# Two decoder layers on one core: layer 0's block attention ahead of its sparse attention

## The chip, the core and the metric

The kernel runs on one core of one Trainium2 chip, as one program with one launch. The metric is the device time in microseconds (us). Matrix products run on TensorE, elementwise work and reductions on VectorE, activations and some copies on ScalarE, a smaller share on GpSimd (POOL in the profile), and the weights come in by DMAs that SyncE (SP) issues.

## The reference, cut to what matters

The input has 256 tokens of 1024 float32 numbers. Two layers follow one another, each a mixer, a cross-attention to 256 memory tokens and a gated feed-forward part, each behind an RMS norm and added to the residual stream. What the change touches is the mixer of layer 0. It has one input projection, two groups of eight heads, and one output projection:

```python
def dsa_moba_mixer(h, positions, w_in, w_out, ...):
    aq, ak, av, iq, ik, iw, bq, bk, bv = _split(h @ w_in, AB_SIZES)
    aq = partial_rope(rms_norm(aq, a_q_norm), positions)
    ak = partial_rope(rms_norm(ak, a_k_norm), positions)
    iq = partial_rope(iq, positions)
    ik = partial_rope(ik, positions)
    o_a = dsa_attention(aq, ak, av, iq, ik, iw)
    bq = partial_rope(rms_norm(bq, b_q_norm), positions)
    bk = partial_rope(rms_norm(bk, b_k_norm), positions)
    o_b = moba_attention(bq, bk, bv)
    return jnp.concatenate([o_a, o_b], axis=-1) @ w_out

def dsa_attention(q, k, v, q_idx, k_idx, w_idx):
    logits = einsum('bqhd,bsd->bqhs', q_idx, k_idx)
    score = einsum('bqh,bqhs->bqs', w_idx, relu(logits))
    score = where(causal, score, NEG_INF)
    _, sel = lax.top_k(score, 64)
    ...
```

Group A is the sparse attention. A small indexer of eight heads scores every key for every query, the 64 best keys are kept, and the eight heads attend to these through one shared key and value head. Group B is the block attention. With 256 tokens there is one block of 256 keys, so it is causal attention with eight key and value heads. The two groups need nothing of one another; their outputs meet in the output projection, whose rows 0 to 511 belong to A and 512 to 1023 to B.

## The kernel before, in words

**Tiles.** The tokens are two tiles (t = 0, 1) of 128. A gemm (L571) multiplies one token tile by one block of up to 512 weight columns into one of two PSUM buffers `mm`. Weights and activations are each split into a high and a low part of the type fp32r, and each product is three matmuls (`mm3`, L565): high by high, high by low, low by high. Eight slices of the 1024 inputs make 24 matmuls of 512 columns for one tile and one block; `both` (L588) runs the two tiles one after the other.

**Weights.** The list `plan` names the order in which weight pieces are loaded; it is filled from `BL0` (L413) for layer 0's input projection and goes on with `mk` (the memory's keys), the output projection `out` in two halves of 512 rows (half 0 is A's, half 1 is B's), `mq`, `mv`, `mo` and the feed-forward part. One piece is 2 slices by up to 512 columns. SyncE loads it into one of three buffers `raw`; `pusher` (L395) then casts it to the high part (mostly on ScalarE) and takes the low part by a subtraction on VectorE, into one of six buffers `whl`. Both token tiles use a piece before its buffer is free. In the trace this subtraction is `whl<-raw,whl`; the prediction calls it a split.

**Layer 0's mixer** (`mixer0`, L750) has five blocks: `s` of 424 columns (shared key and value of A, index queries, keys and weights), `aq`, `bk`, `bq` and `bv` of 512 each. `BL0` and the gemms at the end of `mixer0` have them in this order. Behind each gemm runs an evacuation: `ev_small` (L761) for `s`, `ev_q` (L850) for `aq` and `bq`, `ev_k` (L869) for `bk`, `ev_v` (L892) for `bv`. They scale, rotate and transpose (PSUM buffers `tp`), and write high and low parts into `slab` tiles.

Three loops follow. `index` (L812) computes, tile by tile, the eight index heads' scores on TensorE, ReLU on ScalarE and the weighted sum on VectorE into `acc`. `top` (L839) then runs eight rounds of MAX8 and MATCH_REPLACE on VectorE, each of which takes eight keys out, and turns the result into a mask, `bias`. `attention` (L898) goes through four (group, tile) pairs, four pairs of heads in each. Per pair of heads (`scores`, L692): scores into `sp`; mask and row maximum on VectorE; exponential on ScalarE; scaling; transposes into `tp`; copy to `pt`; product with the values into `po`. `finish` (L741) copies `po` to the two slabs that the output projection reads.

```python
def attention():
    for br, t in ((0, 0), (0, 1), (1, 0), (1, 1)):
        if br == 0:
            yield has(("aqT", t))
            yield has("akT", 2)
            yield has(("bias", t))
```

`br` 0 is A, the sparse attention, and 1 is B. So A's first tile waits for the first tile's top-k, A's second for the second tile's.

**After the mixer** `main` (L1479) runs `mem_k` (block `mk`), then `project` (L1375), which takes half 0 of the output projection for both tiles and then half 1, each with two column blocks, then the cross-attention (`mq` first) and the feed-forward part. `mem_prep` (L1242), the norm and transposes of the memory, is started ahead of the `bv` gemms.

**What sets the order.** All of this is generators that yield one instruction at a time. When the program is built, `Steps` (L84) picks among the instructions that are ready: per engine, of those that could start within 0.03 us of the earliest, the one with the lowest rank. When something could start is estimated by `Est` (L140), with durations from `Engine.cost` (L236) and `Est.issue` (L194). On the chip each engine runs its own queue in the order so fixed. Every instruction is issued by one line, L232 (L237 in the changed kernel), so that the trace tells operations apart by the tiles' names.

## Time and profile before

| what | us |
|---|---|
| median of 3 runs | 803.23 (802.14 to 803.38) |
| the profiled execution | 801.81 |
| its span | 800.1 |
| TensorE busy in it | 766.0 |
| VectorE busy | 537.5 |
| ScalarE busy | 435.4 |

The profile is of one execution. The span runs from the first to the last instruction that it shows; the execution's own time is 1.7 us longer. Busy time is the time in which an engine has an instruction running. A row of the view in time has start, duration and the instruction (output tile, input tiles, shapes, data type), how many like it follow one another, and in brackets how long the engine was idle just before and which engine's work ended that. PEclk is TensorE's granted clock as a share of 2.4 GHz, so that 0.50 is 1.2 GHz.

### The profile page before, as it was taken

The numbers are of one execution on the slowest core, as the hardware profiler recorded it, in microseconds if no ns is written. First come the engines' busy times: TensorE is split into PE (matmuls) and PEld (weight loads), VectorE is DVE, ScalarE is ACT, GpSimd is POOL, SyncE is SP. The second block draws the span as 40 slices with busy tenths as digits, with TensorE's granted clock in tenths as the row PEclk, the third lists the DMA queues.
The fourth block names the chain that finished last, engine by engine and source line by source line (L and its number), as shares of the span: only waits on it lengthen the run. The fifth ranks groups of instructions, "written<-read, shape, count | busy, mean of one in ns | idle before, by whom it ended". The sixth has DMA issues, their size and how long they took to land.

```text
span 800.1 us, 11833 instructions
## 1 busy us (share of the span) xinstructions
PE 766.0 (96%) x4259; PEld 632.1 (79%) x4259; DVE 537.5 (67%) x1096; ACT 435.4 (54%) x816; POOL 130.9 (16%) x192
## 2 busy tenths in 40 slices
PE   6878999999999999999999988999999999999998
PEld 5766777888888888888878776878897888889886
DVE  6779998877655655545727798887868565646541
ACT  5666887565544434444526788864656334435430
POOL 1544332110000000000007463230200000000000
PEclk9999999999999999999999999999999999999999
DMA  7613334635565553887315632033635656546761
GB/s 221 208 55 112 134 124 122 181 119 159 158 191 179 168 186 119 240 251 224 116 56 148 210 112 81 1 103 110 184 105 146 198 184 180 167 141 209 225 184 52
DMA packets 69482, 121.27 MB, mean 152 GB/s; under 512 B 8420, under 2 KB 15664, under 8 KB 69424
## 3 DMA queue, kind: packets, MB, share of 16 engines
q1 hardware_dynamic: 69392, 120.53, 49.2%
q8 instruction: 33, 0.54, 0.3%
q14 instruction: 25, 0.20, 0.1%
q0 software_dynamic: 32, 0.00, 0.0%
HBM read 119.46 MB, written 1.05 MB: 151 GB/s over the span
## 4 chain that ended last, share of the span: by engine, by line
PE 83%; DVE 7%; ACT 4%; DMA 2%; issue 2%; POOL 1%; SPq 0%; POOLq 0%; ACTq 0%; DVEq 0%
PE mm L232 61%; PE po L232 12%; PE tp L232 7%; PE sp L232 3%; DVE whl L232 2%; DMA raw<-in_ab_w_in 1%; DMA raw<-in_ffn_w_in 1%; ACT sn L232 1%; ACT whl L232 1%; DVE slab L232 1%; DVE acc L232 1%; ACT slab L232 1%; DVE sn L232 1%; DVE t L232 1%; POOL sn L232 1%
## 5 line engine op out<-in xcount | busy, mean ns | idle before, releaser
L232 PE MATMUL mm<-whl,h 128*128 128x512 f32 (+3 forms) x1776 | 397.8, 379 | 8.5 <-DVE whl L232 6.9
L232 PEld LDWEIGHTS mm<-whl,h 128*128 128x128 f32 x1776 | 310.8, 189 | 68.0 <-DVE whl L232 8.9
L232 DVE TENSOR_TENSOR whl<-raw,whl 128x1024 fp32r<-128x1024 f32 (+3 forms) x232 | 270.9, 1170 | 116.6 <-ACT whl L232 112.4
L232 ACT ACTIVATE whl<-raw 128x1024 fp32r<-128x1024 f32 (+3 forms) x211 | 213.2, 1014 | 160.1 <-DMA raw<-in_ffn_w_in 38.4
L232 PE MATMUL mm<-whl,slab 128*128 128x512 f32 (+1 forms) x840 | 200.2, 376 | 0.9 <-DVE x L232 0.8
L232 PEld LDWEIGHTS mm<-whl,slab 128*128 128x128 f32 x840 | 140.6, 189 | 27.7 <-issue 2.4
L232 PE MATMUL po<-whl,slab 128*128 128x512 f32 x264 | 68.4, 396 | 0.0
L232 ACT ACTIVATE slab<-tp 128x256 fp32r<-128x256 f32 (+2 forms) x63 | 28.3, 471 | 56.3 <-PE tp L232 55.9
L232 PEld LDWEIGHTS po<-whl,slab 128*128 128x128 f32 x264 | 49.4, 188 | 11.4
L232 POOL TENSOR_TENSOR rh<-vh,mhalf 128x1 f32<-128x1 f32 x12 | 9.5, 794 | 293.6 <-DVE vh L232 283.1
L232 ACT ACTIVATE sn<-sn,mx 128x128 f32<-128x128 f32 (+1 forms) x96 | 42.7, 447 | 6.9 <-DVE mx L232 6.5
L232 PE MATMUL tp<-ident,t 128*128 128x128 f32 x224 | 34.8, 277 | 2.7 <-DVE slab L232 2.3
L232 PE MATMUL tp<-ident,sn 128*128 128x128 f32 (+1 forms) x180 | 30.9, 281 | 4.8 <-POOL sn L232 3.8
L232 DVE TENSOR_TENSOR x<-mm,x 128x512 f32<-128x512 f32 x36 | 24.6, 687 | 16.0 <-PE mm L232 15.9
L232 PEld LDWEIGHTS tp<-ident,t 128*128 128x128 f32 x224 | 27.1, 142 | 9.6 <-DVE slab L232 2.8
L232 ACT ACTIVATE pt<-tp 128x512 f32<-128x512 f32 (+2 forms) x51 | 27.0, 536 | 13.7 <-PE tp L232 11.8
L232 DVE CUSTOM_DVE_ANT_0 sn<-sp,cm,rq 128x128 f32<-128x128 f32 (+1 forms) x80 | 30.5, 410 | 4.9 <-PE sp L232 3.8
L232 POOL TENSOR_TENSOR sn<-sn,rc 128x512 f32<-128x512 f32 (+2 forms) x27 | 25.5, 944 | 43.5 <-DVE rc L232 28.6
L232 ACT ACTIVATE t<-mm,rh 128x512 f32<-128x512 f32 (+1 forms) x26 | 17.0, 654 | 27.0 <-PE mm L232 27.0
L232 PEld LDWEIGHTS tp<-ident,sn 128*128 128x128 f32 (+1 forms) x180 | 20.7, 141 | 11.6 <-POOL sn L232 5.2
L232 ACT ACTIVATE t<-mm 128x512 f32<-128x512 f32 (+2 forms) x46 | 23.7, 553 | 10.0 <-PE mm L232 8.0
L232 DVE SCALAR_TENSOR_TENSOR t<-mm,rh,t 128x512 f32<-128x512 f32 (+1 forms) x24 | 16.9, 704 | 18.2 <-PE mm L232 18.2
(200 smaller groups left out, 676.3 us busy)
## 6 DMA issues: line engine op xcount, KB each, us to landing
raw<-in_ffn_w_in SPq DMA_DIRECT2D x80, 512.0 KB, 3.8
raw<-in_ffn_w_out SPq DMA_DIRECT2D x44, 512.0 KB, 4.5
raw<-in_ab_w_in SPq DMA_DIRECT2D x16, 512.0 KB, 3.9
raw<-in_mem_w_kv SPq DMA_DIRECT2D x16, 512.0 KB, 4.0
raw<-in_nsa_w_in SPq DMA_DIRECT2D x16, 512.0 KB, 3.7
raw<-in_ab_w_out SPq DMA_DIRECT2D x8, 512.0 KB, 3.6
raw<-in_mem_w_q SPq DMA_DIRECT2D x8, 512.0 KB, 4.2
raw<-in_mem_w_o SPq DMA_DIRECT2D x8, 512.0 KB, 3.6
```

Source lines behind the costliest of these rows:

```text
L232: return f(*a, **{q: v() if q in ("start", "stop") and callable(v) else v for q, v in k.items()})
```

## The change

Layer 0's blocks come as `bk`, `bq`, `bv`, `s`, `aq`; the attention takes B's two tiles first and A's second; the output projection takes half 1 (B's rows) first and half 0 second, in the plan of the weights and in `project`. `mem_prep` starts behind `s`. Three things in memory change with it: A's slabs are taken when they are written, not at the start; the index sums and masks lie in a buffer that has the tag of layer 1's `kvT`; and the scratch output of the norm's square is a T2 buffer, not one of its own. `ev_q` and `ev_k` wait for the rotation's tables, whose generator has rank 2 where it had 3. The estimate for TensorE has another price of a matmul, and a price for a change between outputs of up to 64 partitions and wider ones. Both kernels issue the same operations.

```diff
@@ class Est: issue
+            thin = outs[0].shape[0] <= 64
+            if thin != self.thin:
+                t += 0.09
+            self.thin = thin
@@ class Est: Engine.cost
                 if k.get("tile_position", (0, 0))[1]:
-                    return 0.053
+                    return 0.012
                 if ins[0].dtype == F32R:
-                    return n * (1 if n >= 256 else 4) * 0.000422
+                    return n * 0.00043 + 0.009
@@ trunk
-    BL0 = [("s", 512, 424), ("aq", 0, 512), ("bk", 1448, 512), ("bq", 936, 512), ("bv", 1960, 512)]
+    BL0 = [("bk", 1448, 512), ("bq", 936, 512), ("bv", 1960, 512), ("s", 512, 424), ("aq", 0, 512)]
...
-        for half in (0, 1):
+        for half in (1, 0) if L == 0 else (0, 1):
             for c in (0, 1):
                 plan_block((L, "out", half, c), ...
@@ norm, mem_prep
-    junk = tp.tile([P, 512], F32, name="junk")
+        junk, f = yield from T2.get([P, 512])
@@ mixer0
-        aqT = [[SL.take([P, 4, P], F32R) for _ in range(2)] for _ in range(NT)]
-        akT, akf = SL.take([P, 2, SEQ], F32R)
+        rowsT = hp.tile([P, G + 1, SEQ], F32, name="kvT", tag="kvT")
...
-                acc = hp.tile([P, SEQ], F32, name="acc", tag="acc", bufs=2)
+                acc = rowsT[:, t, :]
...
-            b = hp.tile([P, SEQ], F32, name=f"bias{t}")
+            b = rowsT[:, NT + t, :]
...
+                yield has("tables")
                 yield from rope(q, 8, ra[:, t, 2 * j], rb[:, t, 2 * j], HALF)
...
-            for br, t in ((0, 0), (0, 1), (1, 0), (1, 1)):
+            for br, t in ((1, 0), (1, 1), (0, 0), (0, 1)):
...
         for t in range(NT):
-            yield from gemm((0, "s"), t, h[t], KD, ev_small, (("mix0", t), 0))
-        yield from both((0, "aq"), h, KD, ev_q(0, "aqT"))
-        yield from both((0, "bk"), h, KD, ev_k)
-        yield from both((0, "bq"), h, KD, ev_q(1, "bqT"))
-        spawn(mem_prep(0), 2)
-        yield from both((0, "bv"), h, KD, ev_v)
+            yield from gemm((0, "bk"), t, h[t], KD, ev_k, (("mix0", t), 0))
+        yield from both((0, "bq"), h, KD, ev_q(1, "bqT"))
+        yield from both((0, "bv"), h, KD, ev_v)
+        yield from both((0, "s"), h, KD, ev_small)
+        spawn(mem_prep(0), 2)
+        yield from both((0, "aq"), h, KD, ev_q(0, "aqT"))
@@ project
-        for half in range(2):
+        for half in (1, 0) if L == 0 else (0, 1):
@@ the program's start
-    spawn(tables(), 3)
+    spawn(tables(), 2)
```

**The first index scores in TensorE's queue.** In both lists `sp<-ikT,slab` is an index score, `tp` are transposes, and `mm` with `h_113` or `h_114` is the second token tile of `aq`. Before:

```order
L232 MATMUL tp_530<-ident,t_469 128x128 x4
L232 MATMUL sp_544<-ikT,slab_512 128x256 x2
L232 MATMUL tp_556<-ident,t_469 128x128 x4
L232 MATMUL sp_566<-ikT,slab_512 128x256 x2
L232 MATMUL tp_572<-ident,dk 128x128
L232 MATMUL sp_584<-ikT,slab_526 128x256 x2
L232 MATMUL tp_581<-identr,t_542 128x128 x4
L232 MATMUL tp_598<-identr,t_542 128x128 x2
L232 MATMUL sp_602<-ikT,slab_526 128x256 x2
L232 MATMUL tp_598<-identr,t_542 128x128 x2
L232 MATMUL mm_628<-whl_328,h_113 128x512 x2
L232 MATMUL mm_628<-whl_328,h_114 128x512
```

and now:

```order
L237 MATMUL tp_1052<-ident,t_929 128x128 x4
L237 MATMUL mm_1044<-whl_628,h_113 128x512 x2
L237 MATMUL mm_1044<-whl_628,h_114 128x512
L237 MATMUL mm_1044<-whl_628,h_113 128x512 x2
L237 MATMUL tp_1070<-ident,t_994 128x128 x2
L237 MATMUL sp_1071<-ikT,slab_904 128x256 x2
L237 MATMUL tp_1070<-ident,t_994 128x128 x2
L237 MATMUL mm_1044<-whl_628,h_114 128x512
L237 MATMUL mm_1044<-whl_663,h_113 128x512 x2
L237 MATMUL mm_1044<-whl_663,h_114 128x512
L237 MATMUL mm_1044<-whl_663,h_113 128x512
L237 MATMUL sp_1099<-ikT,slab_904 128x256 x2
```

Before, the second tile's `s` is done (`mm_444`, ahead of this piece), and transposes and index scores stand alone until `mm_628`. Now the index scores stand between the matmuls of `aq`, and 138 rows later in the queue.

**The start of half 0 of the output projection in TensorE's queue.** `mm_1285` is the second tile of `mk`, `mm_1476` the first matmul of half 0, `sp<-slab,slab` and `po<-pt` the attention's scores and products (`av` A's values, `bv` B's). Before:

```order
L232 MATMUL sp_1394<-slab_795,slab_952 128x256
L232 MATMUL mm_1285<-whl_1210,slab_1225 128x512
L232 MATMUL po_1194<-pt_1410,av 64x128 x4
L232 MATMUL tp_1443<-ident,sn_1354 128x128 x2
L232 MATMUL tp_1449<-ident,sn_1386 128x128 x2
L232 MATMUL mm_1285<-whl_1210,slab_1226 128x512
L232 MATMUL mm_1476<-whl_1260,slab_1330 128x512
L232 MATMUL sp_1452<-slab_794,slab_952 128x256
L232 MATMUL sp_1452<-slab_796,slab_952 128x256
```

Now `mm_1496` is half 1's last gemm and `mm_1674` half 0's first:

```order
L237 MATMUL mm_1496<-whl_1348,slab_981 128x512
L237 MATMUL tp_1535<-ident,sn_1476 128x128 x2
L237 MATMUL sp_1523<-slab_1011,slab_1292 128x256 x4
L237 MATMUL po_1474<-pt_1536,av 64x128 x2
L237 MATMUL tp_1561<-ident,sn_1483 128x128 x2
L237 MATMUL po_1474<-pt_1562,av 64x128 x2
...
L237 MATMUL sp_1616<-slab_1011,slab_1345 128x256 x4
L237 MATMUL tp_1625<-ident,sn_1550 128x128 x2
L237 MATMUL sp_1631<-slab_1011,slab_1362 128x256 x4
L237 MATMUL po_1474<-pt_1626,av 64x128 x2
L237 MATMUL mm_1674<-whl_1377,slab_1656 128x512 x2
```

Before, half 0 starts among the scores of A's second tile and B's, right behind a matmul of `mk`. Now half 1 stands ahead of it, and between the two only the rows of the attention of A, twelve of them, of which three are left out here.

**VectorE's queue at the second tile's selection.** `MAX m` and `MATCH_REPLACE` with `128x256` are the second tile's rounds, `ISA sn` the mask and maximum of A's first tile, `whl<-raw,whl` a split, `gv` and `slab<-gv` belong to the memory's preparation, `x_72<-mm` is a residual addition. Before:

```order
L232 MAX m_957<-acc 128x8
L232 TENSOR_SCALAR hss<-hss,he 128x8
L232 MATCH_REPLACE acc<-m_957,acc 128x256
L232 TENSOR_TENSOR slab_925<-gv_940,slab_924 128x512
L232 TENSOR_TENSOR whl_945<-raw_880,whl_945 128x1024
L232 MAX m_983<-acc 128x8
L232 TENSOR_TENSOR gv_994<-tp_989,gT 128x512
L232 ISA sn_964,mx<-sp_963,bias_954,rq_130 128x128
L232 ISA mx 128x1
L232 ISA sn_964,mx<-sp_963,bias_954,rq_130 128x128
```

and now:

```order
L237 MAX m_1462<-kvT 128x8
L237 TENSOR_TENSOR x_72<-mm_1425,x_72 128x512
L237 MATCH_REPLACE kvT<-m_1462,kvT 128x256
L237 ISA sn_1476,mx<-sp_1475,kvT,rq_125 128x128
L237 ISA mx 128x1
L237 MAX m_1488<-kvT 128x8
L237 ISA sn_1476,mx<-sp_1475,kvT,rq_125 128x128
L237 ISA mx 128x1
L237 MATCH_REPLACE kvT<-m_1488,kvT 128x256
L237 ISA sn_1483,mx<-sp_1482,kvT,rq_125 128x128
```

The rounds alternate with the masks of A's first tile in both. Before, a split and the memory's preparation stand among them; now a residual addition of half 1 does.

## Rows read from the trace of the kernel before

**Rows 1.** The page, busy us, share of the span and instructions of each engine.

```profile
PE 766.0 (96%) x4259; PEld 632.1 (79%) x4259; DVE 537.5 (67%) x1096; ACT 435.4 (54%) x816; POOL 130.9 (16%) x192
```

**Rows 2.** Busy time by stretch: stretch, length, engines' busy us (instructions), PEclk, DMA share, GB/s.

```profile
22.00:45.00 23.00, 19.33 (x91) 15.26 (x90) 18.57 (x56) 14.05 (x24) 11.69 (x24) 1.00 0.66 197
45.00:50.00 5.00, 2.15 (x15) 1.66 (x15) 4.81 (x13) 3.54 (x9) 0.76 (x4) 0.97 0.12 47
50.00:53.00 3.00, 3.00 (x12) 2.47 (x12) 1.98 (x8) 2.33 (x6) 2.37 (x5) 0.50 0.00 0
53.00:71.00 18.00, 17.78 (x89) 14.26 (x87) 15.84 (x39) 10.49 (x19) 10.66 (x17) 1.00 0.30 88
71.00:79.00 8.00, 4.86 (x23) 3.50 (x24) 7.44 (x22) 5.79 (x11) 4.08 (x5) 1.00 0.23 67
79.00:97.00 18.00, 16.33 (x100) 12.64 (x100) 16.25 (x64) 14.02 (x34) 7.23 (x11) 1.00 0.37 128
97.00:152.00 55.00, 54.88 (x344) 43.08 (x343) 48.13 (x125) 41.15 (x98) 15.15 (x16) 1.00 0.43 131
...
480.00:500.00 20.00, 16.74 (x166) 13.76 (x166) 17.13 (x73) 16.38 (x53) 7.37 (x9) 1.00 0.22 81
```

**Rows 3.** TensorE's rows in time: start us, us, instruction, count [idle before <-releaser].

```profile
27.00 0.45 PE L232 MATMUL tp<-slab,one 76*128 76x112 f32 x2 [2.05 <-DVE slab L232]
27.21 12.83 PE L232 MATMUL mm<-whl,h 128*128 128x512 f32 x55
...
43.64 1.09 PE L232 MATMUL tp<-ident,t 128*128 128x128 f32 x8 [1.58 <-DVE slab L232]
...
75.06 1.67 PE L232 MATMUL mm<-whl,h 128*128 128x512 f32 x6 [1.54 <-DVE whl L232]
...
152.02 2.96 PE L232 MATMUL mm<-whl,h 128*128 128x512 f32 x12
```

**Rows 4.** VectorE's instructions by form, 0 to 200 us: count | busy us, mean ns | idle before.

```profile
L232 DVE TENSOR_TENSOR whl<-raw,whl 128x1024 fp32r<-128x1024 f32 x45 | 55.2, 1230 | 5.2 <-ACT whl L232 5.0
L232 DVE TENSOR_TENSOR x<-mm,x 128x512 f32<-128x512 f32 x15 | 10.2, 687 | 3.0 <-PE mm L232 2.9
...
L232 DVE TENSOR_SCALAR rc<-rc 128x2 f32<-128x2 f32 x16 | 3.9, 250 | 0.2
L232 DVE SCALAR_TENSOR_TENSOR acc<-sn,iw,acc 128x256 f32<-128x256 f32 x7 | 3.7, 526 | 0.3 <-ACT sn L232 0.3
...
L232 DVE CUSTOM_DVE_ANT_0 sn<-sp,bias,rq 128x256 f32<-128x256 f32 x8 | 3.7, 476 | 0.0
...
L232 DVE MAX8 m<-acc 128x8 f32<-128x256 f32 x8 | 3.3, 416 | 0.0
L232 DVE MATCH_REPLACE8 acc<-m,acc 128x256 f32<-128x256 f32 x8 | 3.2, 406 | 0.0
...
L232 DVE CUSTOM_DVE_ANT_0 sn<-sp,bias,rq 128x128 f32<-128x128 f32 x8 | 2.4, 342 | 0.0
L232 DVE SCALAR_TENSOR_TENSOR acc<-sn,iw,acc 128x128 f32<-128x128 f32 x7 | 2.4, 346 | 0.1
L232 DVE MAX8 m<-acc 128x8 f32<-128x128 f32 x8 | 2.3, 282 | 0.8 <-POOL acc L232 0.8
L232 DVE MATCH_REPLACE8 acc<-m,acc 128x128 f32<-128x128 f32 x8 | 2.2, 272 | 0.0
```

**Rows 5.** VectorE's rows in time, three from 86 us on.

```profile
86.04 0.34 DVE L232 CUSTOM_DVE_ANT_0 sn<-sp,bias,rq 128x128 f32<-128x128 f32 x1
86.31 0.08 DVE L232 DVE_READ_ACCUMULATOR2_ANT mx<- 128x1 f32 x1
86.31 0.34 DVE L232 CUSTOM_DVE_ANT_0 sn<-sp,bias,rq 128x128 f32<-128x128 f32 x1
```

**Rows 6.** ScalarE's instructions by form, 0 to 200 us, columns as in Rows 4.

```profile
L232 ACT ACTIVATE sn<-sn,mx 128x256 f32<-128x256 f32 x16 | 8.0, 503 | 1.3 <-DVE mx L232 1.3
...
L232 ACT ACTIVATE slab<-po 128x512 fp32r<-128x512 f32 x4 | 2.4, 588 | 0.0
```

More of the change, by code (lines that the diff above doesn't have):

```diff
@@ L145, in __init__ @@
         self.wr, self.rd, self.busy = {}, {}, {}
+        self.thin = False
         self.now = 0.0
@@ L630, in norm @@
         ss = tiny(2, "ss")
+        junk, f = yield from T2.get([P, 512])
         for h in range(2):
             yield S.activation(junk, x[t][:, 512 * h:512 * h + 512], AF.Square, accum_out=ss[:, h:h + 1])
+        f()
         vr[key, t] = yield from ms_root(ss, "h", 0, t)
@@ L750, in mixer0 @@
     def mixer0():
-        aqT = [[SL.take([P, 4, P], F32R) for _ in range(2)] for _ in range(NT)]
-        akT, akf = SL.take([P, 2, SEQ], F32R)
-        bqT, bkT, iqT = {}, {}, {}
+        akT, akf = [], []
+        aqT, bqT, bkT, iqT = {}, {}, {}, {}
         ikT = hp.tile([P, SEQ], F32R, name="ikT")
+        rowsT = hp.tile([P, G + 1, SEQ], F32, name="kvT", tag="kvT")
         av = hp.tile([P, NT, HD], F32, name="av")
@@ L807, in ev_small @@
             cf()
+            if t == 0:
+                a, f = yield from SL.get([P, 2, SEQ], F32R)
+                akT.append(a)
+                akf.append(f)
+            yield lambda: akT
             yield from keys_T(lambda i: dk.rearrange("p a d -> p (a d)"), 1,
-                              [(0, 1, akT[:, 0:1, t * P:(t + 1) * P], akT[:, 1:2, t * P:(t + 1) * P])], kv[:, 0:1])
+                              [(0, 1, akT[0][:, 0:1, t * P:(t + 1) * P], akT[0][:, 1:2, t * P:(t + 1) * P])], kv[:, 0:1])
             done("akT")
@@ L855, in ev @@
                 free()
+                yield has("tables")
                 yield from rope(q, 8, ra[:, t, 2 * j], rb[:, t, 2 * j], HALF)
                 def dst(i):
-                    if j == 0:
-                        return aqT[t][i][0]
-                    bqT[t, i] = yield from SL.get([P, 4, P], F32R)
-                    return bqT[t, i][0]
+                    o = (bqT if j else aqT)[t, i] = yield from SL.get([P, 4, P], F32R)
+                    return o[0]
                 yield from stack_T(q, dst)
@@ L874, in ev_k @@
             free()
+            yield has("tables")
             yield from rope(q, 8, ra[:, t, 3], rb[:, t, 3], HALF)
@@ L921, in attention @@
                         hh = 2 * u + i
-                        qs = (aqT[t][hh // 4] if br == 0 else bqT[t, hh // 4])[0][:, hh % 4, :]
+                        qs = (bqT if br else aqT)[t, hh // 4][0][:, hh % 4, :]
                         for e in range(2):
                             yield T.matmul(sp[:, i * SEQ:(i + 1) * SEQ], qs,
-                                     akT[:, e, :] if br == 0 else bkT[e, hh // 2][0][:, hh % 2, :],
+                                     akT[0][:, e, :] if br == 0 else bkT[e, hh // 2][0][:, hh % 2, :],
                                      start=(e == 0), stop=(e == 1))
@@ L935, in attention @@
                 for i in range(2):
-                    (aqT[t][i] if br == 0 else bqT[t, i])[1]()
-            akf()
-            for e in range(2):
-                for i in range(4):
-                    bkT[e, i][1]()
+                    (aqT[t, i] if br == 0 else bqT[t, i])[1]()
+                if br and t:
+                    for e in range(2):
+                        for i in range(4):
+                            bkT[e, i][1]()
+            akf[0]()
         h = [hsel(t) for t in range(NT)]
@@ L977, in mixer1 @@
         gt = [hp.tile([P, G * HG, 3], F32, name=f"gt{t}") for t in range(NT)]
-        kvT = hp.tile([P, G + 1, SEQ], F32, name="kvT")
+        kvT = hp.tile([P, G + 1, SEQ], F32, name="kvT", tag="kvT")
         kbd = hp.tile([P, G, 2, NCMP], F32, name="kbd")
@@ L1250, in mem_prep @@
                 rs = raw[:, 512 * h:512 * h + 512]
+                junk, f = yield from T2.get([P, 512])
                 yield S.activation(junk, rs, AF.Square, accum_out=ss[:, h:h + 1])
+                f()
                 hi = yield from SL.get([P, 4, P], F32R)
```

## The prediction

> **What bounds the kernel now.** The page's busy times come first. TensorE is busy 766.0 of 800.1 us [rows 1], so it is the bound, and whatever is to be won lies in the 34 us in which it waits and in the stretches in which its clock is low. The change reorders layer 0's mixer, so I read the busy time by stretch next [rows 2], cut where the picture changes. From 97 to 152 us, where attention and gemms are mixed, TensorE waits for 0.12 us in all: nothing can be won there. From 22 to 97 us it waits 3.67, 2.85, 0, 0.22, 3.14 and 1.67 us, together 11.5 us, and from 50 to 53 us the granted clock is 0.50, the lower of the two levels. The rest of layer 0 and all of layer 1 are not touched by the new sequence.
>
> The TensorE rows name what it waited for [rows 3]: the tables' matmul at 27.00 (2.05 us, VectorE), the transposes of the index queries from 43.64 on (VectorE's second halves of the slabs) and a weight split at 75.06 (1.54 us). All are VectorE's, which is busy 4.81 of 5 and 7.44 of 8 us there [rows 2]: it has the index sums, the top-k and the evacuations of bk and bq at the same time, and the splits that feed the gemms queue behind them.
>
> **What the change moves.** Nothing is added or removed on any engine that is worth a term: the square's output goes to a t2 slot, the index sums to a buffer that layer 1 uses later, and both are written by the same instructions. What changes is what stands beside what. Now bk, bq and bv come first. Their evacuations run beside 144 gemm matmuls that need nothing but splits, and the splits no longer queue behind a top-k. So I take away all **11.5 us** of waits between 22 and 97 us, and the slow clock with them: 3 us at half rate are **1.5 us** of work. Two things stay of it.
>
> The tables' matmul still stands in the first block, now after 11 of the second tile's matmuls, and VectorE reaches its operand behind six splits as before it did behind eight. I leave 1.2 of the 2.05 us [rows 3]; the ends are 0 and 2.05.
>
> The block attention's first tile now runs while the s block is TensorE's only cover. Where the other attention's first tile ran, from 79 to 97 us, TensorE waited 1.67 us in 18 us [rows 2]; the new stretch, up to the first index score, is about 24 us, which makes 2.2 us. With the 0.12 us of the mixed stretch that follows as the lower end, I take **2 us**; as upper end twice that, 4.4, because ScalarE gets the weight casts of s and aq in the same stretch.
>
> The first block has 512 columns instead of 424, so each of the first four loads is a fifth larger. TensorE gets a fifth more work out of each, which has to be done anyway: I take 0, with 1.8 us as the upper end (four loads of 0.09 MB more each, at the 197 GB/s of the stretch from 22 us on [rows 2]).
>
> **The new seam.** The sparse attention's first tile now has only aq, mk and the output projection's half 1 as cover, and in the order of TensorE nothing but 12 rows of small matmuls stands between half 1 and the first matmul of half 0. That matmul waits for a chain that starts at the first index score, and both sides of it can be counted in the order.
>
> VectorE's side, from the first sum over index heads to the fourth mask-and-max of the second tile, the last one that stands ahead in its queue: 122 instructions and 16 match loads. By the rows of these forms [rows 4]: 9 splits of 1.230 us are 11.1; 7 and 7 index sums of 0.526 and 0.346, 6.1; 8 and 8 MAX8 of 0.416 and 0.282, 5.6; 8 and 8 match-replaces of 0.406 and 0.272, 5.4; 8 and 4 mask-and-max steps of 0.342 and 0.476, 4.6; 16 match loads and 11 reads of the maximum, at the 0.08 of a read [rows 5], 2.2; 4 residual additions of 0.687, 2.7. Of the other 40, 13 are of 512 elements, at the same 0.687, 8.9, and 27 small, at the 0.250 of the reciprocals' clamp, 6.8. The sum is 53.4. These are durations, and instructions overlap at their ends: masks of 0.34 us start 0.27 us apart [rows 5], so I take 0.07 us off for each of the 138, and get 44 us back to back. VectorE will also wait in it. Between 45 and 97 us it was busy for 46.3 of 52 us [rows 2], which would make 5.4 us of waits; much of that belonged to the bk and bq evacuations, which are over by then, so I take 2, with 0 and 5.4 as ends. Ahead of it stand the score's matmul and ScalarE's ReLU, about 0.8 us, and behind it two exponentials and the copy of the attention's output (0.503 twice and 0.588 [rows 6]) with their hand-overs, about 2.2. The chain is 49 us.
>
> TensorE's side of the same stretch: 115 gemm matmuls, at the 12.83/55 = 0.233 us of an undisturbed run of them [rows 3], 26.8 us; and 99 small ones. Between 97 and 152 us, 140 gemm matmuls (32.6 us) and 204 small ones filled 54.88 us [rows 2], which leaves 0.109 us for a small one: 10.8. Together 37.6 us. So TensorE waits 49 - 37.6 = **11.4 us** in the seam. The lower end is 5 (no waits of VectorE, small matmuls at the 0.15 us that they take in short groups), the upper 15.
>
> The waits in the seam are of the kind that cost the clock before. From 45 to 50 us TensorE was busy 2.15 us of 5, with no single wait over 1.6 us, and from 50 to 53 the clock was at 1.2 GHz [rows 2, 3]; that came to 1.5 us, and I take **1.5 us** again, with 0 and 3 as ends. A rule of the Trainium skill would leave this term out: its page "TensorE: Matmul & The Clock Gate", Part 1, says that the half rate is what an idle engine falls back to and that activity releases it. By that rule a seam in which attention matmuls keep coming would stay at 2.4 GHz, and the time would be 1.5 us lower; the row shows the clock falling in such a stretch, so I keep the term.
>
> After the seam, the second tile's attention must be done before the second tile's projection: from the first matmul of half 0 to there TensorE has 24 gemm and about 40 small matmuls, some 10 us, and VectorE 10 splits, masks and copies of about 8 us; this I take as covered.
>
> **Layer 1.** The other TensorE estimate changes the scheduler's choices there too. The order shows the same instructions in groups of nearly the same sizes; the attention from 480 us on waits 3.3 us in 20 [rows 2]. I take 0, with 2 us either way.
>
> **The sum.** The profiled execution took 801.81 us (its span is 800.1). -11.5 - 1.5 + 1.2 + 2 + 11.4 + 1.5 = +3.1: 804.9. The median of the three runs, 803.23, is 1.4 above the profiled one, so I predict **806.3 us**: the waits don't go, they move behind the top-k, and a little is added. A difference of 0.2%, 1.6 us, is about what a measurement of this kernel can tell from none.
>
> **Rivals.** *Faster:* the seam is short. VectorE, rid of the evacuations, runs its chain without waits, the small matmuls take their longer price, the clock stays up, and the two remainders are halved: -13 + 0.6 + 1 + 5.4 = -6, 797.2 us. For it speaks that VectorE has slack ahead of the first score; against it, that the chain starts only there, whatever slack there was. It decides at a seam of 6.7 us, below which the sum is under -1.6. Chance 0.28. *No difference:* a seam of 9 to 10 us with the clock up, -13 + 3.2 + 9.5 = -0.3, 802.9 us. For it speaks that VectorE has about the same work as before ahead of the second projection, in either order. Chance 0.22. *Slower by much:* ScalarE becomes the bound under the block attention, since exponentials, weight casts and the evacuation of s meet there; the first index score comes 4 us late, VectorE waits in its chain as before (a seam of 14), and the clock is low twice: -13 + 1.2 + 4 + 14 + 3 = +9.2, 812.4 us. For it speaks that ScalarE was busy 41.15 of 55 us in the mixed stretch [rows 2]; against it, that TensorE hardly waited there. Chance 0.12.
>
> **How the numbers follow.** The forecast has 0.38; with the last rival, slower has 0.50; no difference 0.22; faster 0.28. The range reaches from 799 (a seam of 7 us, no low clock, the small terms halved: -4.4) to 812, which leaves out the far ends of the first and the last rival, about 2 in 10. The forecast alone is 804 to 809.
>
> **What would show it.** Right: TensorE's waits between 25 and 80 us are under 5 us in all, and the clock stays up there; the first index score comes at about 80 to 86 us; a stretch of some 12 us ahead of half 0's first matmul, at 125 to 137 us, in which TensorE is busy for less than half and waits for scaled probabilities, VectorE is above 90%, and the clock falls once; mq's first matmul comes at about 154 us instead of 152.02 [rows 3]. Wrong: half 0 follows half 1 with under 6 us of waits, or waits for splits remain under bq and bv, or layer 1 differs by more than 2 us.

## The result, and the profile after

The changed kernel takes **814.04 us** (median of 4 runs, 812.3 to 815.96) against 802.93 of the kernel before (median of 4 runs): a ratio of 1.0137, 95% interval 1.0119 to 1.0155. It is slower by 11 us, where 3 were forecast, and outside the range. The profiled execution took 812.63 us.

The page's first row and its row of TensorE's clock (tenths of full speed in 40 slices of 20 us), after:

```profile
PE 772.3 (95%) x4259; PEld 633.9 (78%) x4259; DVE 536.8 (66%) x1093; ACT 432.6 (53%) x816; POOL 133.9 (17%) x195
...
PEclk9999987999999999999999999999999999999999
```

TensorE has as many instructions as in [rows 1] and is busy for 6.3 us more. VectorE has three instructions fewer and GpSimd three more. The clock shows a dip at slices 6 and 7; before, all 40 slices are at 9. Busy time in four stretches tells where the 11 us are: up to mq's first matmul, to layer 1's first gemm, to layer 1's mk, and the rest (columns as in [rows 2]). Before:

```profile
0.00:152.02 152.02, 133.20 (x732) 105.45 (x732) 125.72 (x358) 103.82 (x218) 55.83 (x94) 0.99 0.46 140
152.02:388.50 236.48, 234.60 (x1190) 196.63 (x1188) 145.50 (x190) 113.48 (x164) 6.95 (x9) 1.00 0.60 179
388.50:500.00 111.50, 103.34 (x740) 85.22 (x738) 77.29 (x223) 71.27 (x178) 48.10 (x68) 0.98 0.41 123
500.00:800.10 300.10, 294.87 (x1604) 244.82 (x1603) 189.04 (x329) 146.83 (x260) 20.00 (x23) 1.00 0.47 146
```

After:

```profile
0.00:157.61 157.61, 136.90 (x731) 108.14 (x732) 127.33 (x359) 104.48 (x218) 58.78 (x93) 0.95 0.43 135
157.61:395.50 237.89, 235.64 (x1190) 196.58 (x1188) 143.05 (x185) 114.27 (x167) 8.70 (x11) 1.00 0.60 179
395.50:508.70 113.20, 103.69 (x742) 85.10 (x742) 79.54 (x227) 68.13 (x173) 45.89 (x69) 1.00 0.39 120
508.70:810.90 302.20, 296.11 (x1600) 244.08 (x1599) 186.89 (x324) 145.69 (x261) 20.50 (x24) 1.00 0.46 145
```

Layer 0 up to mq is 5.6 us longer. TensorE's waits there grew by 1.9 us only (157.61 - 136.90 against 152.02 - 133.20); its busy time for the same work grew by 3.7, with the clock at 0.95 in place of 0.99. The other three stretches, where the prediction had 0, are 1.4, 1.7 and 2.1 us longer, together 5.2. Over the whole span, 10.8 us longer, TensorE waits 4.5 us more.

Inside layer 0, TensorE's rows in time (columns as in [rows 3]):

```profile
23.08 0.45 PE L237 MATMUL tp<-slab,one 76*128 76x112 f32 x2 [2.02 <-DVE slab L237]
...
85.40 0.48 PE L237 MATMUL sp<-ikT,slab 128*128 128x256 f32 x2
...
103.68 0.72 PE L237 MATMUL tp<-identr,t 128*128 128x128 f32 x4 [5.24 <-DVE t L237]
...
131.11 0.44 PE L237 MATMUL tp<-ident,sn 128*128 128x128 f32 x2 [0.97 <-POOL sn L237]
...
137.93 1.22 PE L237 MATMUL mm<-whl,slab 128*128 128x512 f32 x2 [0.70 <-ACT slab L237]
```

and the same stretch in steps of 1 us:

```profile
100.00:101.00 1.00, 0.00 (x0) 0.00 (x0) 0.00 (x0) 1.00 (x2) 1.00 (x1) 1.00 0.23 88
101.00:102.00 1.00, 0.00 (x0) 0.00 (x0) 0.86 (x2) 0.60 (x2) 1.00 (x2) 0.52 0.00 0
...
107.00:108.00 1.00, 1.00 (x5) 0.67 (x4) 0.97 (x5) 0.71 (x2) 0.00 (x0) 0.57 0.00 0
...
130.00:131.00 1.00, 0.14 (x4) 0.00 (x0) 0.96 (x6) 0.83 (x5) 0.55 (x1) 1.00 0.00 0
131.00:132.00 1.00, 0.44 (x2) 0.20 (x2) 0.88 (x2) 1.00 (x3) 0.06 (x1) 0.88 0.00 0
...
141.00:142.00 1.00, 1.00 (x5) 0.90 (x4) 1.00 (x3) 0.65 (x2) 0.00 (x0) 0.50 0.00 0
142.00:143.00 1.00, 1.00 (x8) 0.71 (x9) 0.80 (x3) 0.19 (x1) 0.17 (x1) 1.00 0.50 104
```

and the seam, its first part and the work behind it as a whole:

```profile
128.00:138.00 10.00, 6.80 (x36) 4.46 (x35) 9.21 (x35) 7.38 (x24) 3.51 (x4) 0.69 0.31 107
128.00:132.00 4.00, 1.85 (x13) 0.80 (x12) 3.84 (x17) 3.09 (x12) 1.23 (x2) 0.97 0.01 4
138.00:142.00 4.00, 4.00 (x13) 3.00 (x14) 4.00 (x8) 3.65 (x8) 1.04 (x1) 0.50 0.44 131
```

The first index score comes at 85.40, as forecast. The long waits for splits and for the index queries that stood at 43 to 78 us [rows 3] are gone. Two things stand in their place. One is a wait of 5.24 us that no step of the prediction had; the other is the seam ahead of half 0 (137.93), with 3.2 us of waits from 128 to 138. In each the clock falls to 1.2 GHz, and it stays there for work that follows, from 101 to 107.9 and from 131.8 to 142 us. Summed over steps of 1 us, busy time times one minus the granted clock, the low clock costs 6.6 us up to mq here and cost 1.7 before. Over the whole span it is 6.6 against 3.4.

The first wait, read on the engines it waits for: VectorE (first three rows) and ScalarE.

```profile
99.28 0.68 DVE L237 TENSOR_TENSOR gv<-tp,gT 128x512 f32<-128x512 f32 x1
101.14 0.69 DVE L237 TENSOR_REDUCE hss<-t 128x4 f32<-128x512 f32 x1 [1.18 <-ACT t L237]
...
102.85 0.69 DVE L237 TENSOR_TENSOR t<-t,t 128x512 fp32r<-128x512 f32 x1
```

```profile
98.89 0.62 ACT L237 ACTIVATE t<-t 128x512 f32<-128x512 f32 x1
...
99.99 0.63 ACT L237 ACTIVATE slab<-gv 128x512 fp32r<-128x512 f32 x1 [0.39 <-DVE gv L237]
100.53 0.58 ACT L237 ACTIVATE t<-mm 128x512 f32<-128x512 f32 x1
```

TensorE's next row needs the low part that VectorE writes at 102.85. Ahead of it in VectorE's queue stands mk's evacuation (`hss`, 101.14), which waits for ScalarE's copy of mk (100.53), and that stands behind the memory's square and slab (98.89, 99.99). The memory's preparation, which starts behind `s` now, so ends up ahead of the index queries on two engines.

### The profile page after: what moved, and what is told of

Its sections match the earlier page's. It is cut to its first block, busy times and chain, and to the rows that moved or that the text cites. A ratio compares the mean times of both kernels' runs of the same rounds, so it can differ in the third digit from the quotient of the medians.

```text
span 810.9 us, 11849 instructions
## 1 busy us (share of the span) xinstructions
PE 772.3 (95%) x4259; PEld 633.9 (78%) x4259; DVE 536.8 (66%) x1093; ACT 432.6 (53%) x816; POOL 133.9 (17%) x195
## 4 chain that ended last, share of the span: by engine, by line
PE 71%; DVE 12%; DMA 6%; ACT 6%; issue 3%; POOL 1%; SPq 0%; ACTq 0%; DVEq 0%; POOLq 0%
PE mm L237 52%; PE po L237 11%; PE tp L237 6%; DVE whl L237 4%; PE sp L237 2%; ACT whl L237 2%; DVE sn L237 2%; DMA raw<-in_ffn_w_in 1%; ACT sn L237 1%; DMA raw<-in_ab_w_in 1%; DMA raw<-in_nsa_w_in 1%; DVE t L237 1%; DVE kvT L237 1%; DMA raw<-in_ffn_w_out 1%; ACT t L237 1%
## 5 line engine op out<-in xcount | busy, mean ns | idle before, releaser
L237 ACT ACTIVATE whl<-raw 128x1024 fp32r<-128x1024 f32 (+2 forms) x208 | 210.0, 1014 | 163.2 <-DMA raw<-in_ffn_w_out 45.4
L237 PEld LDWEIGHTS mm<-whl,slab 128*128 128x128 f32 x840 | 142.5, 190 | 30.9 <-ACT mvm L237 2.2
L237 ACT ACTIVATE slab<-tp 128x256 fp32r<-128x256 f32 (+2 forms) x71 | 30.6, 460 | 52.1 <-PE tp L237 51.8
L237 PEld LDWEIGHTS po<-whl,slab 128*128 128x128 f32 x264 | 49.2, 188 | 11.7
L237 ACT ACTIVATE sn<-sn,mx 128x128 f32<-128x128 f32 (+1 forms) x96 | 42.6, 447 | 10.6 <-DVE mx L237 10.0
L237 ACT ACTIVATE h<-gv 128x512 fp32r<-128x512 f32 x22 | 13.8, 628 | 27.4 <-DVE gv L237 27.4
L237 DVE CAST whl<-raw 128x1024 fp32r<-128x1024 f32 (+2 forms) x24 | 18.1, 754 | 15.2 <-PE mm L237 13.0
```

The lines of the kernel that those rows point to most:

```text
L237: return f(*a, **{q: v() if q in ("start", "stop") and callable(v) else v for q, v in k.items()})
```

## The experiments

Every "us over before" below is the ratio of that run to the runs of the kernel before on the same chip, less 1, times 802.

### The change taken apart: e1, e2, e3, e5 to e8

The change has four parts that can be set singly: the memory edits (slots, slabs, buffer), the tables' rank, the estimate, and the order of layer 0. Seven kernels and the change itself make all combinations on top of the memory edits. For e1 the estimate is as before:

```diff
-                t += 0.09
+                t += 0.0
-                    return 0.012
+                    return 0.053
-                    return n * 0.00043 + 0.009
+                    return n * (1 if n >= 256 else 4) * 0.000422
```

> The change with the three numbers of the TensorE estimate as they were; order of the blocks, memory and start as in the change. Theory (the 11 us have two sources: the mixer of layer 0, in which mq's first matmul comes 5.6 us later because of two stretches at the lower clock, and the estimate, whose other choices cost 5.2 us from there to the end): about 809 us, mq's first matmul still 4 to 7 us late, the rest of the program as in the kernel before. Rival (the later 5 us come from the order or the memory): 813 to 815. Rival (the estimate makes the stalls in layer 0 too): 803 to 805.

For e2 the order is as before:

```diff
-    BL0 = [("bk", 1448, 512), ("bq", 936, 512), ("bv", 1960, 512), ("s", 512, 424), ("aq", 0, 512)]
+    BL0 = [("s", 512, 424), ("aq", 0, 512), ("bk", 1448, 512), ("bq", 936, 512), ("bv", 1960, 512)]
-            for br, t in ((1, 0), (1, 1), (0, 0), (0, 1)):
+            for br, t in ((0, 0), (0, 1), (1, 0), (1, 1)):
...
-        for half in (1, 0) if L == 0 else (0, 1):
+        for half in (0, 1):
```

> The change with layer 0's order undone (blocks, attention, halves of the output projection, start of the memory's preparation); the new estimate and the memory edits stay. Theory (order costs 5.6 us, estimate 5.2): about 808 us, mq's first matmul at 152 us give or take 2. Rival (all of it is the order): 802 to 804. Rival (all is the estimate): 813 to 815.

e3 has both of these edits.

> Only the memory edits, the wait for the tables and the tables' rank are left of the change: order and estimate as before. Theory (they cost nothing, as the prediction took it): 802 to 804 us. Rival (the buffer that index sums share with layer 1, or the T2 slot of the square, holds something up in the later part): 807 to 809.

Measured: e1 810.68 us (1.0113, 1.0091 to 1.0134), e2 811.02 (1.0106, 1.0084 to 1.0128), e3 806.48 (1.0059, 1.0042 to 1.0076). Neither the order nor the estimate is the whole of it, and the 4.7 us of e3 were expected by the rival alone. Of the edits that are left in e3, those in memory move nothing: e5 has these alone (rank 3, and no wait for the tables), and in its trace every engine's instructions have the order of before. That leaves the tables' rank and the wait for them; e6 to e8 keep the wait. The next four have it at 3:

```diff
-    spawn(tables(), 2)
+    spawn(tables(), 3)
```

> The kernel before with the memory edits alone: A's slabs taken when written, index sums and masks in the buffer with the tag of layer 1's, the square in a T2 slot. The tables' generator keeps rank 3. Every engine's queue then has the same instructions in the same order as before (operands apart). Theory (the 5 us of the run with memory edits and tables come from the tables' rank, which reorders the queues from the start of the program): 801 to 803 us, no difference from before. Rival (a buffer holds something up): 806 to 808.

> The change with the tables' generator at rank 3 as before. Theory (parts add up: rank 5 us, order 4, estimate 4): about 809 us. Rival (no part has a price of its own; each other order of the queues just has its own one or two stalls, and the order of the blocks decides what the longest can be): anywhere from 803 to 815, with stalls of over 2 us at other places than in the change.

> The new order of layer 0 with memory edits, but the old estimate and the tables at rank 3. This is what the prediction was about, with its seam. Prediction's own forecast for the order: 3 us over before, 804 to 805. Theory (parts add up): 806. Rival (each order has its own stalls): anywhere from 802 to 812; the stretch ahead of half 0 waits 3 to 8 us in any case, and the clock falls there.

> The new estimate with memory edits; the old order of layer 0 and the tables at rank 3. Prediction's own term for the estimate: 0, with 2 us either way. Theory (parts add up): 806 us, mq's first matmul within 2 us of before and the rest later in layer 1. Rival (each order has its own stalls): 800 to 810, with the difference already there at mq's first matmul.

| parts, beside the memory edits | run | us over before | with rank 2 | us over before |
|---|---|---|---|---|
| none | e5, 1.0030 | 2.4 | e3 | 4.7 |
| order | e7, 1.0068 | 5.5 | e1 | 9.1 |
| estimate | e8, 1.0089 | 7.1 | e2 | 8.5 |
| both | e6, 1.0132 | 10.6 | the change | 11.0 |

Each part's price is the mean of four differences: order 3.0, 4.3, 3.4 and 2.5, mean **3.3**; estimate 4.7, 3.8, 5.1 and 1.9, mean **3.9**; rank 2.3, 3.6, 1.4 and 0.4, mean **1.9**; the memory edits **2.4**, one difference. They add up to 11.5, near the 11.0 of the change; each difference carries some 2 us of uncertainty. The order includes the later start of the memory's preparation, and the rank may hang on the estimate (2.3 and 3.6 with the old one, 1.4 and 0.4 with the new). For e5 the theory fell: the edits that leave every queue as it was are not free (interval 1.0017 to 1.0043). For the others the parts add up within their uncertainty, and the rival of no prices at all isn't needed for the sums.

By place, in one profiled execution of each, the parts do not add up. Up to mq's first matmul the order costs 0.7, 2.0, 2.0 and 3.0 us in its four pairs. But the rank costs 4.9 and 6.3 us there with the old estimate, and nothing with the new (-0.9 and 0.1). From layer 1's first gemm to the last matmul it is 407.8 us before, 408.6 in e5, and 409.6 to 411.6 in the seven kernels that have all of the new estimate, whose TensorE queues are the same in layer 1. But e7, with the old estimate, needs 412.4 there, with the clock low from 472 to 480 and 486 to 490, so that most of its price stands where the order changes nothing. The prices hold for the sum alone; where each is lost isn't shown.

### Is any other order of the queues slower? e11, e12

If the kernel before merely had a fortunate order, a change of the estimate that says nothing would cost as much as a real one. e11 raises one price by half a per cent, e12 lowers it by as much:

```diff
-                    return n * (1 if n >= 256 else 4) * 0.000422
+                    return n * (1 if n >= 256 else 4) * 0.000424
```

> The kernel before with one price of the estimate half a per cent higher (a matmul's 0.000422 us per column becomes 0.000424), which says nothing new of the chip but gives the queues another order from the third block on. Theory (the kernel before is an order that happens to have few stalls; any other loses some us, the new estimate and the tables' rank too): 803.5 to 808 us. Rival (the new estimate's numbers are bad as such, and a neutral one is free): 801 to 803.

> As the run before, with the price half a per cent lower (0.000420), which gives a third order. Theory: 803.5 to 808 us. Rival: 801 to 803.

Measured: 802.48 us (1.0004, 0.9994 to 1.0015) and 801.83 (0.9990, 0.9980 to 1.0000), though both move instructions on every engine. My theory fell: these two orders cost nothing, so another order is not dear as such. Whether the estimate's new numbers cost for what they say, or have led to a less fortunate order than these two, is not shown; the tables' rank, which says nothing of durations, is not free either.

### The estimate's numbers, and the square's slot: e13, e14, e15

e13 is the kernel before with the last of e1's three lines in its new form, e14 with the other two; e15 is the kernel before with the square in a T2 slot:

```diff
+        junk, f = yield from T2.get([P, 512])
         for h in range(2):
             yield S.activation(junk, x[t][:, 512 * h:512 * h + 512], AF.Square, accum_out=ss[:, h:h + 1])
+        f()
```

> The kernel before with the new matmul price alone (0.00043 us per column and 0.009: 0.229 us for 512 columns, 0.064 for 128, where it was 0.216 and 0.216). Theory (this is the number that costs: it makes narrow matmuls cheap against the splits that they stand between, so that TensorE's queue takes weights sooner than VectorE has split them, as in the waits of 1.5 us near 443 us in all runs with the new estimate): 805 to 808 us, with a wait of about 1.5 us for a split between 435 and 447 us. Rival (the price for the change of output widths and the one of the value products cost): 801 to 803.

> The kernel before with the other two numbers alone: 0.09 us at a change between outputs of up to 64 partitions and wider ones, and 0.012 us in place of 0.053 for a value product. Theory of the run before: 801 to 803 us. Its rival: 805 to 808 us; if both runs lie at 803 to 805 the cost is split between them, and if neither costs, it is the pair of them that does.

> The kernel before with one memory edit alone: the square's output goes to one of the four T2 slots instead of a tile of its own. Queues in the same order. Theory (the run with all memory edits was 2.5 us over before because ScalarE's square must wait until such a slot is read out, which holds up what is queued behind it on ScalarE): 803.5 to 805.5 us. Rival (it is A's slabs or the shared buffer): 801 to 803.

Measured: e13 805.11 us (1.0032, 1.0020 to 1.0044), e14 803.94 (1.0017, 1.0006 to 1.0028), e15 804.42 (1.0031, 1.0016 to 1.0046). The matmul price costs 2.6 us and the other two numbers 1.4, together as much as the estimate above. The mechanism that I had expected for e13 is not what its trace shows. The wait near 443 us belongs to all three numbers together (e8, and the change at 444.97):

```profile
443.17 4.17 PE L237 MATMUL mm<-whl,h 128*128 128x304 f32 x15 [1.54 <-DVE whl L237]
```

With the matmul price alone, there is none there, and two others stand elsewhere:

```profile
75.06 1.91 PE L232 MATMUL mm<-whl,h 128*128 128x512 f32 x5 [3.04 <-DVE whl L232]
...
472.04 1.12 PE L232 MATMUL tp<-ident,sn 128*128 128x128 f32 x4 [2.54 <-POOL sn L232]
```

But the price of e13 is not in its waits. The first of them takes the place of two, 1.54 us at 75.06 [rows 3] and 1.30 at 78.03 before, and mq's first matmul comes at 151.7, no later than before:

```profile
78.03 1.19 PE L232 MATMUL mm<-whl,h 128*128 128x512 f32 x4 [1.30 <-DVE whl L232]
```

By e13's page TensorE waits for 32.5 us of 804.1, where it waited 34.1 before, and is busy for 5.6 us more:

```profile
PE 771.6 (96%) x4259; PEld 633.8 (79%) x4259; DVE 532.9 (66%) x1087; ACT 434.1 (54%) x821; POOL 137.2 (17%) x196
```

The low clock is 1.5 of these, by the same sum as above; why the same matmuls take the other 4 us isn't shown. The square's slot is as dear as all memory edits together (1.0031 against 1.0030, each give or take 1 us). Where that is lost isn't shown either: e15's profiled execution took 801.62 us, its shortest, and has no new wait.

### The seam and the first wait: e4, e9, e10

e4 puts the memory's value gemm between the halves, as cover:

```diff
         for half in (1, 0) if L == 0 else (0, 1):
+            if L == 0 and half == 0:
+                yield from mem_v(0)
             for t in range(NT):
```

> The change, with the memory's value gemm (96 matmuls of 256 columns, about 11 us of TensorE) moved from behind mq to between half 1 and half 0 of layer 0's output projection, weights' plan included. Theory (half 0 waits for A's first tile: 3.2 us of waits from 128 to 138 us, and the clock at its lower level from 131.9 to 142 us, another 4.2): both go, 806 to 808 us, granted clock 1.00 from 120 to 150 us. Rival (the value gemm was cover for the memory attention's softmax, which then waits): 811 to 814 us, with new waits of 4 us or more behind mq. Rival (the low clock comes from something else than the waits): the clock still falls near 132 us, 810 to 812.

Measured: 817.16 us (1.0185, 1.0155 to 1.0216), above every expectation, though the rival named the place. The seam is mostly covered (from 120 to 150 us TensorE is busy for 28.00, though the clock still falls, to 0.94 on the mean), and the memory attention now waits for its own softmax, longer than the seam did:

```profile
187.21 1.65 PE L237 MATMUL sp<-mkT,slab 128*128 128x256 f32 x6 [3.97 <-ACT sn L237]
```

e9 starts the memory's preparation earlier:

```diff
         yield from both((0, "bq"), h, KD, ev_q(1, "bqT"))
+        spawn(mem_prep(0), 2)
         yield from both((0, "bv"), h, KD, ev_v)
         yield from both((0, "s"), h, KD, ev_small)
-        spawn(mem_prep(0), 2)
```

> The change, with the memory's preparation started behind the bq gemms (as early as before) instead of behind s. Theory (TensorE's wait of 5.24 us that ends at 103.68 comes from the memory's preparation and mk's evacuation, which stand ahead of the index queries' low part on ScalarE and VectorE): no wait over 2 us between 90 and 115 us and no lower clock there, mq's first matmul at 150 to 153 us, 806 to 809 us. Rival (each order has its own stall, wherever it is): another wait of over 2 us with the lower clock behind it, 811 to 815.

Measured: 809.22 us (1.0094, 1.0072 to 1.0117), 3.4 us less than the change, give or take 2. The wait of 5.24 us and the low clock behind it are gone, so the theory of its cause holds; but mq starts at 155.7, not at 150 to 153. The seam got worse, and its low clock, from 121 to 142 us, costs 8.3 us:

```profile
121.69 1.19 PE L237 MATMUL sp<-slab,slab 128*128 128x256 f32 x4 [2.91 <-DVE mx L237]
```

e10 leaves out half of the selection's rounds, so that each query keeps 32 keys and not 64:

```diff
-            for i in range(DSA_TOP // 8):
+            for i in range(DSA_TOP // 16):
```

> The change with 4 of the 8 rounds of the selection left out in each tile (each query keeps 32 keys, not 64). By the prediction's chain (half 0 waits for VectorE's index sums, rounds and masks) 4 rounds of both tiles are 16 instructions and 8 match loads less, about 5 us of VectorE: the waits from 128 to 138 us (3.2 us) go and with them the lower clock (4.5 us), mq's first matmul 4 to 8 us earlier, 806 to 810 us; the wait that ends at 103.68 stays, since it is ahead of the rounds. Rival (the seam is the hand-overs of A's attention itself, from ScalarE to GpSimd to TensorE and back, as the brackets at 128 to 138 us name them): the waits stay at 2 to 4 us and the clock falls as in the change, 812 to 815.

Measured: 805.26 us (1.0031, 1.0019 to 1.0043), 8.5 us less than the change and below what was expected. TensorE does not wait at all in the seam's stretch, the clock stays up there, and mq starts at 151.8:

```profile
105.07 0.72 PE L237 MATMUL tp<-identr,t 128*128 128x128 f32 x4 [5.24 <-DVE t L237]
```

```profile
120.00:150.00 30.00, 30.00 (x185) 22.61 (x184) 26.66 (x81) 18.97 (x53) 7.62 (x9) 1.00 0.30 94
```

The first wait is still there, as expected. So half 0 waits for VectorE's chain, as the prediction had it, although the brackets of the change's rows at 131 us name GpSimd: that is the last link, not the slow one. Leaving out 16 instructions and 8 match loads on VectorE, about 5 us, brings mq 5.8 us earlier: up to there TensorE waits 3.6 us less, and the low clock costs 3.7 in place of 6.6.

### The order by itself: e16, e17, e18

e16 has the new order, with most of what else the change brought taken off: old estimate, rank 3, the square in a tile of its own, and the preparation started as in e9. A's slabs, the shared buffer and the wait for the tables stay.

> The new order of layer 0 without what else the change brought: old estimate, tables at rank 3, the square in a tile of its own, and the memory's preparation behind bq. From the medians so far: order, slabs and buffer 807.7, less 2.5 for the square, less up to 4.8 for the preparation: 800.5 to 805 us. Theory (the order alone costs what the seam ahead of half 0 costs): 803 to 806, and the seam with the lower clock stays between 120 and 145 us. Rival (without the other edits the order is a gain): under 800.

Measured: 804.39 us (1.0027, 1.0017 to 1.0036), 2.2 us over before. The two rows are the stretch from the first index score to half 0's first matmul, first e16's, then the change's:

```profile
86.90:135.16 48.26, 38.56 (x221) 29.64 (x220) 46.43 (x146) 30.90 (x69) 15.89 (x20) 0.96 0.35 110
```

```profile
85.40:137.93 52.53, 43.94 (x223) 34.95 (x222) 47.31 (x148) 32.66 (x72) 21.14 (x28) 0.88 0.30 101
```

In e16 TensorE is busy for 38.56 us of 48.26, VectorE for 46.43; mq starts at 154.2, and the low clock costs 1.6 us up to there. That is the prediction's chain (49 us), cover (37.6), clock (1.5) and mq (154). But the waits, 9.7 us where 11.4 were forecast, stand at two places, since VectorE's residual additions, which free a PSUM buffer, also queue behind the selection:

```profile
111.67 0.50 PE L237 MATMUL mm<-whl,slab 128*128 128x512 f32 x1 [3.14 <-DVE x L237]
...
129.90 0.44 PE L237 MATMUL tp<-ident,sn 128*128 128x128 f32 x2 [3.26 <-POOL sn L237]
```

e17 and e18 move `s` forward in e16, to start the selection earlier, in the list and in the gemms alike; both start the preparation behind the third block, ahead of `bv`, where e16 has it behind the second. e17's order:

```diff
-    BL0 = [("bk", 1448, 512), ("bq", 936, 512), ("bv", 1960, 512), ("s", 512, 424), ("aq", 0, 512)]
+    BL0 = [("bk", 1448, 512), ("s", 512, 424), ("bq", 936, 512), ("bv", 1960, 512), ("aq", 0, 512)]
```

> As the order without the other edits (e16), but with the blocks bk, s, bq, bv, aq: the selection starts some 35 us earlier, under bq and bv, while B's attention still comes first and half 1 before half 0. Theory (what the order costs is the seam: half 0 waits for a chain on VectorE that starts at the first index score): the waits of 9.9 us between 100 and 160 us fall to under 3, a part comes back as waits for splits between 40 and 80 us (before has 9 of them there), 799 to 803 us. Rival (VectorE has too much work ahead of half 0 in any order, so the waits only move): 803 to 806 us.

> As e17 with the blocks bk, bq, s, bv, aq: the selection starts some 20 us earlier than in e16. Theory: between e17 and e16, or better than both if the waits for splits stay small: 798 to 804 us, the waits between 100 and 160 us at 2 to 6. Rival: 803 to 806.

Measured: 805.91 us (1.0044, 1.0027 to 1.0061) and 807.13 (1.0071, 1.0049 to 1.0092). The rival holds: the waits of e17 move and do not shrink to the 3 us of the theory. e18 lies above its rival's range too. First e17, then e18:

```profile
22.00:100.00 78.00, 73.89 (x407) 59.37 (x406) 68.38 (x203) 58.13 (x123) 45.83 (x67) 1.00 0.47 145
100.00:152.00 52.00, 43.65 (x256) 32.72 (x255) 42.49 (x118) 30.13 (x73) 13.53 (x14) 0.96 0.32 105
```

```profile
22.00:100.00 78.00, 74.63 (x433) 61.26 (x433) 66.57 (x181) 58.75 (x128) 47.07 (x68) 1.00 0.48 145
100.00:152.00 52.00, 42.02 (x234) 32.29 (x228) 44.16 (x138) 25.32 (x61) 10.47 (x11) 0.87 0.30 101
```

From 22 to 152 us TensorE waits 12.5 us in e17 and 13.4 in e18; by the same two stretches 12.3 in e16, 12.3 in the change and 11.7 before. VectorE is busy for 109 to 114 of these 130 us in all five. Up to mq's first matmul the rows are these, for e16, e17 and e18:

```profile
0.00:154.23 154.23, 134.11 (x731) 105.75 (x732) 129.95 (x365) 99.11 (x211) 63.59 (x91) 0.99 0.46 140
0.00:157.97 157.97, 137.22 (x732) 106.90 (x732) 127.43 (x358) 103.31 (x217) 63.59 (x94) 0.98 0.44 138
0.00:156.86 156.86, 135.89 (x732) 108.09 (x733) 128.71 (x363) 100.28 (x214) 61.99 (x93) 0.96 0.44 136
```

TensorE waits 20.1, 20.8 and 21.0 us there, 20.7 in the change and 18.8 before. Where the selection stands sets where TensorE waits, and hardly how long. What differs more is the low clock: 1.6 us in e16, 3.3 in e17, 4.1 in e18, 6.6 in the change. No version with the new order beats the kernel before.

## Why the prediction was wrong

**What held.** The waits of the first part go and come back behind the selection. From 25 to 80 us TensorE waits for 1.8 us in the change, and the first index score comes in time. In e16 the chain, TensorE's cover, the clock and mq came out as worked out, at +2.2 us (1.4 to 2.9) where +3.1 was forecast; the tables' matmul still waits, 2.02 us in the change where 1.2 was left. That half 0 waits for VectorE is shown by e10. That the mean of the four pairs, 3.3 us, lies nearer to +3.1 is in part luck: it includes the late preparation, which the forecast had not, and in e7 layer 1's low clock. (The prediction's own sum would put mq at 155.1; the 154 that it names is not worked out from it.)

**What failed: the terms set to 0.** "I take 0, with 2 us either way" for the estimate was 3.9, twice the bound. It was argued from groups of nearly the same sizes in the order, which says nothing of what stands ahead of what. That "both are written by the same instructions" took the square's slot as free; it costs 2.4 to 2.5 (e5, e15). The tables' rank had no term: it moves instructions on every engine from the program's start, and costs about 1.9 on the mean. These three are 8 of the 11 us, and in none of them is an instruction added. The runs show the prices; by what wait or at what matmuls they are lost stays open. The prediction's own mark of being wrong here, layer 1 off by more than 2 us, came up: its two stretches are 3.8 us longer.

**What failed: the memory's preparation.** That it starts behind `s` was left out of the sum. Its rows on ScalarE and VectorE make the wait of 5.24 us; e9, in which the wait is gone, shows that they do.

**What failed: the seam and the clock.** In the change only 3.2 us of waits stand between half 1 and half 0, where 11.4 were forecast and under 6 was named as a sign of being wrong. 1.5 us of low clock was forecast for the seam, with 3 as the upper end, and 1.5 taken away; 6.6 was measured in the change against 1.7 before, 4.5 of it at the seam. The low clock stays for work that follows the waits: 131.8 to 142 us for 3.2 us of waits from 128 to 138. Not every bundle of waits brings it: 3.14 us of waits from 71 to 79 us before left the clock at 1.00 [rows 2]. The prediction chose the row against the rule of the Trainium skill's page "TensorE: Matmul & The Clock Gate", Part 1, that activity releases the half rate. The trace agrees with the choice: the clock fell in a stretch in which attention matmuls kept coming. In the wait of 5.24 us, in which TensorE did nothing, it fell as the page has it.

**The rivals.** *Slower by much*, 812.4 us at a chance of 0.12, is nearest in time and had the clock low twice, but its cause was another: ScalarE did not become the bound under the block attention (from 53 to 85.4 us TensorE waits for 2.0), and the index score was not late. *Faster* and *no difference* are out: even e16's interval lies above 1. No rival had a price for parts that only move instructions.

## What to carry to other kernels

In a list-scheduled kernel, each number of the cost estimate and each rank is an edit of its own: give it a term with a range taken from an experiment, and separate it from the edit that it comes with. Where one engine has work for most of a stage (VectorE, 109 to 114 of 130 us here), reordering the stage moves the other engine's waits and hardly shortens them; what pays is less work on the engine that fills the stage (e10). A wait's price is the wait and the low clock that may come with it, so one bundle of waits may cost twice its length: the seam's 3.2 us of waits came with 4.5 of low clock.

## What the runs showed that was not expected

A better fit made a slower kernel: the new matmul price gives 0.229 us for 512 columns, nearer to the 0.233 of an undisturbed run [rows 3] than the old 0.216, and costs 2.6 us, while two neutral steps of half a per cent cost nothing. It costs them with fewer waits of TensorE, not more (e13).

The clock stays low through full work: in the change TensorE is busy throughout from 138 to 142 us and its granted clock is 0.50 until 142; it fell at 131.8, after waits in which TensorE was busy for 1.85 us from 128 to 132. And an output tile that takes a slot of a rotating pool instead of a tile of its own costs 2.5 us with every queue in the same order; by what wait stays open.
